# The last pass of the attention scores over 128 rows instead of 64

## The chip, the cores and the metric

The kernel runs on one core of one Trainium2 chip. The metric is the device time of one execution in microseconds; the number of record is the median of the runs, and beside it stands a profiled execution, whose span runs from the program's first instruction to its last.

The engines are named as in the profile: PE is TensorE's matmuls (transposes are matmuls with an identity), PEld its weight loads, DVE is VectorE, ACT is ScalarE, POOL is GpSimd, SP is the engine that issues most DMAs.

## What is computed

The reference is an encoder of two layers over 1024 tokens of 1024 channels in float32. Each layer has a token mixer (attention with four heads beside a depthwise convolution of width 31), an output projection, and a feed-forward part with 16 experts, each of which takes its 128 best tokens. The change lies in the attention. Per head a query and a key have 192 channels: 128 plain ones, and 64 that are rotated by the token's position. In the reference, in short:

```
q = concatenate([q[..., :QK_NOPE_DIM], apply_rope(q[..., QK_NOPE_DIM:], cos, sin)], axis=-1)
k = concatenate([k[..., :QK_NOPE_DIM], apply_rope(k[..., QK_NOPE_DIM:], cos, sin)], axis=-1)
...
s = einsum('bhqd,bhkd->bhqk', q_blk, kt) * scale
p = softmax(s, axis=-1)
return einsum('bhqk,bhkd->bhqd', p, vt)
```

with `QK_NOPE_DIM = 128`, 64 rotated channels, and the same rotated key channels for all heads but for their scale.

## The kernel before

**High and low parts.** Most products take their operands as float32r, which holds fewer bits than float32. So an operand x is kept as a high part, `hi` (x rounded by ScalarE's copy), and a low part, `lo` = x - `hi` (made by VectorE); `split` (L118, L119) does this. A product is three passes of TensorE into the same accumulator, hi hi, lo hi and hi lo (`mm3`, L113 to L115).

**The rotated channels** have only 64 rows, so two of their passes are packed into one of 128 rows. `q_t` (L525) writes `qs`: its rows 0 to 63 are the high part of the rotated query, rows 64 to 127 the low part. `k_t` (L517) writes `kd`, in which the high part of the rotated key stands twice, in rows 0 to 63 and again in 64 to 127, and `kl`, the low part, in rows 0 to 63 alone. Both go through `out_r` (L512): ScalarE copies all 128 rows to `hi` (L514), VectorE subtracts in the rows `r` it is given (L515). For both the source `p2` holds the rotated values twice, in both halves of its rows.

**The scores** of a tile of 128 queries (`scores(u)`, L540) are two halves of 512 keys. For each half there are five passes: three for the plain channels (L113, L114, L115), then `qs` by `kd` over 128 rows (L548: high query by high key, and low query by high key), then rows 0 to 63 of `qs` by rows 0 to 63 of `kl` (L549: high query by low key). A call thus has ten passes, of which two have 64 rows.

**The order of the attention.** Each engine issues in the order in which the program is written; nothing is reordered by a planner. The loop over u (L862) goes over 32 tiles, four heads of eight. In the step of tile u VectorE takes the reciprocal of tile u's sum (L866), and the maximum of tile u + 1's scores (L554, L555); TensorE transposes the probabilities of tile u (`probs_t`, L571, eight transposes in two buffers that ScalarE copies out, L572), and multiplies those of tile u - 1 by the values (`values`, L578); ScalarE takes the exponential of tile u + 1 (L564) behind the copy of the output of tile u - 1 (L579). At the end of the step TensorE does `scores(u + 2)`. So scores, maximum, exponential and transposes of a tile are spread over three steps. Into the steps of the first three heads the next head's queries and keys are woven (`k_mm`, `k_out`, `k_scale`, `k_t`, `q_mm`, `q_out`, `q_rot`, `q_t`; transposes L504, outputs L509, L510, L514, L515), and products of the convolution by VectorE (`give`, L304). Twice a head `values_t` transposes four output tiles and splits them (L118, L119). In the last head there is none of that; in its place come the convolution's layer norm (`ln_in`, transposes L595, statistics by VectorE and three operations of GpSimd; `ln_out` by ScalarE, L606) and the splitting of the output projection's weights (`split_wo`).

Score accumulators (`ps_s`) have two buffers, and so have the two other kinds of accumulators (`ps_t`, `ps_m`).

Of the kernel before, what the change touches and what calls it, by code (L numbers as in the profile page):

```python
# [10 lines left out]
F32 = mybir.dt.float32  # L11
# [9 lines left out]
T, D, KT, TT = 1024, 1024, 8, 8  # L21
# [16 lines left out]
# words per partition of the two arenas  # L38
# [4 lines left out]
def trunk(ctx: ExitStack, tc: tile.TileContext, x, c, positions, norm1_g, w_ada, b_ada, w_in, q_latent_g, w_uq,  # L43
# [10 lines left out]
    ctx.enter_context(tc.manual_schedule())      # each engine issues in the order of this program  # L54
# [5 lines left out]
    # R without the places of two kinds of data, float32 and float32r by turns  # L60
# [15 lines left out]
    class Cut:  # L76
        """[128, 8, n] in two places"""
# [43 lines left out]
    # ---------------------------------------------------------------- constants  # L121
# [17 lines left out]
    # vectors that are needed with their index on the partitions  # L139
# [27 lines left out]
    # columns of b_ada: shift 1, scale 1, shift 2, scale 2  # L167
# [21 lines left out]
    # rotary tables: cos [p, t, 32] and sin with its sign [p, t, (-, +) 32]  # L189
# [31 lines left out]
    # ---------------------------------------------------------------- DRAM scratch  # L221
# [6 lines left out]
    # constants of the router  # L228
# [12 lines left out]
    # ---------------------------------------------------------------- modulation  # L241
    AB = [consts.tile([128, 4, KT], F32, name=f"ab{l}") for l in range(L)]   # scale, shift of the first norm, the second

    def mod_load(l, n, h, raw):
        """rows 512 h .. 512 h + 511 of the columns 512 n .. 512 n + 511 of the modulation of layer l"""
        sp.dma_start(raw, w_ada[l].rearrange("(k p) f -> p k f", p=128)[:, 4 * h:4 * h + 4, 512 * n:512 * n + 512])
# [24 lines left out]
    # ---------------------------------------------------------------- one layer  # L271
    SCR, CB, VB, WRAW, FX = 6144, 8960, 14240, 16288, 28672

    # taps of the depthwise convolution that the parts of the program take
    TAPS = [[1, 0, 2, 0, 2, 2, 2, 1], [1, 1, 2, 1, 1, 1, 0, 1], [3, 6, 5], [4, 4], [0, 0, 7, 9, 7, 5, 5, 8], [5, 6], [5, 6], [0, 0, 8, 8, 6, 4, 6, 5], [[], 0, 1], [0], 1, 1, 0]

    def layer(l):
# [13 lines left out]
        # per token: eps * mean square of the q latent + eps^2, 1 / rms of the kv latent, its square, sum of k rope^2  # L291
        tok = consts.tile([128, 4, TT], F32, name=f"tok{l}", tag="tok")
        RQ = {}
        taps = []                  # depthwise convolution, one product per entry, given out between other work
# [12 lines left out]
        # ---- h = rms_norm(x) * A + B, transposed, in two parts of 512 tokens  # L307
# [23 lines left out]
        # ---- convolution input, gated: y[channel, 15 + token]  # L331
# [27 lines left out]
        # ---- latents: [token, q 256 | kv 128 | k rope 64]  # L359
# [41 lines left out]
        def rotate(dst, src, gr, t0):  # L401
            """dst [128, 4, n, 64] (n copies) = rotated src [128, 4, 64] * gr, for the tokens of tiles t0 .. t0 + 3"""
            xg, xc, xs_ = (fw(o, 4, 64) for o in (SCR + 2304, SCR + 2560, 17280))
            v.tensor_tensor(xg, src, gr[:, None, :].to_broadcast([128, 4, 64]), op=MUL)
            half = lambda ap: ap.rearrange("p t (a b) -> p t a b", a=2)
            v.tensor_tensor(half(xc), half(xg), rc[:, t0:t0 + 4, None, :].to_broadcast([128, 4, 2, 32]), op=MUL)
            v.tensor_tensor(half(xs_), half(xg)[:, :, ::-1], rs[:, t0:t0 + 4], op=MUL)
            if dst.shape[2] == 1:
                v.tensor_tensor(dst[:, :, 0], xc, xs_, op=ADD)
            else:  # L410
                v.tensor_tensor(dst, xc[:, :, None, :].to_broadcast(list(dst.shape)),
                                xs_[:, :, None, :].to_broadcast(list(dst.shape)), op=ADD)
# [5 lines left out]
        # ---- heads  # L418
# [31 lines left out]
        def q_out(hd, grp):  # L450
            st = small.tile([128, 4], F32, name="qst")
            for i in (0, 2):
                a.activation(qr[:, i:i + 2], QS[hd, grp][i // 2][:, :2 * DH].rearrange("p (a b) -> p a b", a=2), AF.Copy)
            for i in range(4):
                jk = small.tile([128, 256], BF16, name="jk", bufs=1)
                a.activation(jk[:, :DH], qr[:, i], AF.Square, accum_out=st[:, i:i + 1])
            tg = slice(4 * grp, 4 * grp + 4)
            # the scale of the exponential carries 1 / sqrt(DH) and 1 / rms(q)
            g.tensor_scalar(st, st, 1.0 / DH, None, op0=MUL)
            g.tensor_tensor(st, st, tok[:, 0, tg], op=ADD)  # L460
            g.tensor_tensor(st, st, neghalf.to_broadcast([128, 4]), op=ALU.pow)
            g.tensor_scalar(RQ[hd][:, tg], st, 1.0 / math.sqrt(DH), None, op0=MUL)
# [54 lines left out]
        def k_t(hd, grp, pool=ps_t):  # L517
            kn, kd, kl, _ = kv_tiles(hd)
            kr, kr2 = kbuf(hd, grp)
            p = to_heads(lambda i: kr[:, i], pool)  # L520
            p2 = to_heads(lambda i: flat(kr2[:, i]), pool)
            out_n(p, kn, grp, c_gk(l))
            out_r(p2, kd, kl, slice(0, 64), grp)
# [10 lines left out]
        # ---- scores, softmax, values  # L534
# [5 lines left out]
        def scores(u):  # L540
            hd, qt = divmod(u, TT)
            kn, kd, kl, _ = kv_tiles(hd)
            qsl = slice(128 * qt, 128 * qt + 128)
            ps = SC[u] = ps_s()
            for n in range(2):
                s = slice(512 * n, 512 * n + 512)
                mm3(ps[:, s], qn[0][:, qsl], qn[1][:, qsl], kn[0][:, s], kn[1][:, s], True, False)
                pe.matmul(ps[:, s], qs[:, qsl], kd[:, s], start=False, stop=False)  # L548
                pe.matmul(ps[:, s], qs[:64, qsl], kl[:64, s], start=False, stop=True)  # L549
# [7 lines left out]
        def exp_table():  # L557
            """an exponential ahead of those that count: the engine loads its table for it"""
            a.activation(small.tile([128, 1], F32, name="ss")[:1], ident[:1, :1], AF.Exp)
# [21 lines left out]
        def values_t(u):  # L581
            """the outputs of the four tiles that end with u, transposed"""
            hd, grp = divmod(u // 4, 2)
            p = to_heads(lambda i: att(u - 3 + i))
            s = slice(512 * grp, 512 * grp + 512)
            split(catA[0][:, hd, s], catA[1][:, hd, s], p)

        # ---- layer norm of the convolution over the channels, swish
# [33 lines left out]
        # ---- output projection  # L622
# [12 lines left out]
        # ================ order: first norm, convolution input  # L635
# [3 lines left out]
        S = [_view(XC["C"], 2048 * i, (4, 512)) for i in range(4)]       # of the first layer  # L639
# [45 lines left out]
        def mod_now():  # L685
            """the next 512 columns; what mod_then() does needs their sums"""
# [108 lines left out]
        # ================ latents  # L795
# [14 lines left out]
        # ================ the rest of the convolution input, first head  # L810
# [50 lines left out]
        # ================ attention  # L861
# [67 lines left out]
        # ================ output projection, residual, second norm, router logits  # L929
# [45 lines left out]
        # weights of the experts, in parts of 2 x 128 rows, of which each is two blocks of 512 columns  # L975
# [8 lines left out]
        # the part that takes the place of another once that is split  # L984
# [9 lines left out]
        # the last ones in halves  # L994
# [26 lines left out]
        def split_lo(c, q):  # L1021
            """the low part of a quarter of the weights, by the tensor engine"""
# [11 lines left out]
        # ---- router: the CAP first tokens of each expert.  The CAP-th largest affinity of an expert is found from  # L1034
        # its eight sorted lists of 128 tokens, merged to the CAP largest.  Lists are sorted in quarters.  Of the
        # lists of two tiles the first lies in the partitions 0 .. 15, the second in 16 .. 31.
# [7 lines left out]
        def bitonic(n, src, nxt, d):  # L1044
            """sorts each bitonic run of 2 d in the first n partitions, downwards"""
# [10 lines left out]
        def sort_tiles(t0, nt, dst=None, dst2=None):  # L1056
            """sorted lists of the tiles t0 .. t0 + nt - 1, 16 partitions each"""
# [30 lines left out]
        def merge(a_, b_, dst, dst2):  # L1088
            """the largest of two lists, 32 partitions"""
            steps.append(lambda: v.tensor_tensor(dst[:32], a_, b_[:, ::-1], op=ALU.max))  # L1090
            return bitonic(32, dst, dst2, 64)
# [19 lines left out]
        def affine(t):  # L1111
            """softmax of the router's logits, rstd * (x A2 Wr) + B2 Wr"""
# [103 lines left out]
        # what a slot takes from its token: index within the tile, tile, affinity in three exact parts  # L1216
# [26 lines left out]
        # slot of a chosen token: the chosen ones before it; of the tokens at the threshold the first ones are chosen.  # L1243
        # before: those at least at the threshold before the token; after: those above it, from the token on
# [52 lines left out]
        # ================ experts  # L1297
# [101 lines left out]
    # ---------------------------------------------------------------- program  # L1399
# [27 lines left out]
```

## Time and profile before

| what | value |
|---|---|
| runs, us | 2357.45, 2357.79, 2359.66 |
| median, us | 2357.79 |
| profiled execution, span, us | 2356.6 |
| what lies around that span, from the median, us | 1.2 |
| TensorE busy, share of the span | 96% |
| VectorE busy, share of the span | 81% |
| ScalarE busy, share of the span | 58% |
| attention of the first layer, us from the span's start | 238 to 456 |
| attention of the second layer, us | 1396 to 1614 |
| mean granted TensorE clock | 0.988 |

The profile gives no device time of its own for the profiled execution; its span is what is compared with the runs. A busy engine is not an engine at its peak: TensorE's matmuls overlap each other, so their durations add up to more than the time that passes. How fast a row of matmuls goes is read from the distance between their starts.

### The profile page before, as it was taken

The numbers are of one execution on the slowest core, as the hardware profiler recorded it, in microseconds if no ns is written. First come the engines' busy times: TensorE is split into PE (matmuls) and PEld (weight loads), VectorE is DVE, ScalarE is ACT, GpSimd is POOL, SyncE is SP. The second block draws the span as 40 slices with busy tenths as digits, with TensorE's granted clock in tenths as the row PEclk, the third lists the DMA queues.
The fourth block names the chain that finished last, engine by engine and source line by source line (L and its number), as shares of the span: only waits on it lengthen the run. The fifth ranks groups of instructions, "written<-read, shape, count | busy, mean of one in ns | idle before, by whom it ended". The sixth has DMA issues, their size and how long they took to land. (4 is left out here: it accounts for less than half of the span.)

```text
span 2356.6 us, 31226 instructions
## 1 busy us (share of the span) xinstructions
PE 2259.5 (96%) x11845; PEld 1789.3 (76%) x11845; DVE 1907.4 (81%) x2648; ACT 1356.9 (58%) x1770; POOL 416.8 (18%) x405
## 2 busy tenths in 40 slices
PE   6999999999999999999969999999989999999997
PEld 3678788787688787878847778877867887787786
DVE  3886888567888999999959868875688889999997
ACT  4324666623667677776741356666246667677675
POOL 1001211201021222313010021121010121331320
PEclk9999999999999999999979999999999999999999
DMA  8472000344899999999946300004358999999996
GB/s 271 157 258 77 13 9 1 109 146 153 302 338 352 371 382 380 373 387 377 354 137 211 131 12 15 1 28 155 116 208 314 344 349 387 379 379 382 373 386 236
DMA packets 179355, 550.97 MB, mean 234 GB/s; under 512 B 12821, under 2 KB 34471, under 8 KB 179205
## 3 DMA queue, kind: packets, MB, share of 16 engines
q1 hardware_dynamic: 169712, 515.35, 59.0%
q0 software_dynamic: 9216, 33.56, 5.6%
q8 instruction: 93, 1.52, 0.3%
q14 instruction: 58, 0.47, 0.1%
q10 hardware_dynamic: 276, 0.07, 0.0%
HBM read 515.35 MB, written 33.59 MB: 233 GB/s over the span
## 5 line engine op out<-in xcount | busy, mean ns | idle before, releaser
L119 DVE TENSOR_TENSOR R<-F,R 128x2048 fp32r<-128x2048 f32 (+1 forms) x294 | 635.9, 2182 | 74.7 <-ACT R L118 74.3
L118 ACT ACTIVATE R<-F 128x2048 fp32r<-128x2048 f32 (+1 forms) x294 | 532.9, 1832 | 71.2 <-DMA F<-in_w_up_dram 26.9
L115 PE MATMUL S<-R,flexX 128*128 128x512 f32 x1096 | 431.9, 394 | 9.8 <-DVE R L119 9.8
L113 PE MATMUL S<-R,flexX 128*128 128x512 f32 x1096 | 439.0, 401 | 0.0
L114 PE MATMUL S<-R,flexX 128*128 128x512 f32 x1096 | 427.3, 390 | 0.0
L304 DVE SCALAR_TENSOR_TENSOR F<-F,cw 128x1024 f32<-128x1024 f32 x240 | 307.4, 1281 | 5.3
L119 DVE TENSOR_TENSOR flexC<-F,flexC 128x2048 fp32r<-128x2048 f32 (+3 forms) x126 | 257.9, 2052 | 16.9 <-ACT flexC L118 16.9
L115 PEld LDWEIGHTS S<-R,flexX 128*128 128x128 f32 x1096 | 205.6, 188 | 64.0 <-DVE R L119 16.8
L118 ACT ACTIVATE flexC<-F 128x2048 fp32r<-128x2048 f32 (+3 forms) x126 | 216.8, 1728 | 47.1 <-DMA F<-in_w_in_dram 14.0
L114 PEld LDWEIGHTS S<-R,flexX 128*128 128x128 f32 x1096 | 206.1, 188 | 42.7
L113 PEld LDWEIGHTS S<-R,flexX 128*128 128x128 f32 x1096 | 206.1, 188 | 39.6 <-ACT flexX L118 0.5
L118 ACT ACTIVATE flexX<-T 128x512 fp32r<-128x512 f32 x128 | 73.1, 597 | 237.3 <-PE T L1314 133.6
L115 PE MATMUL S<-R 128*128 128x512 f32 x480 | 189.9, 396 | 0.0
L113 PE MATMUL S<-flexC,flexX 128*128 128x512 f32 x440 | 176.5, 401 | 0.0
L115 PE MATMUL S<-flexC,flexX 128*128 128x512 f32 x440 | 173.3, 394 | 2.5 <-DVE flexC L119 2.5
L114 PE MATMUL S<-flexC,flexX 128*128 128x512 f32 x440 | 171.8, 390 | 2.4 <-DVE flexX L119 2.4
L1359 POOL DMA_INDIRECT x<-F,idx x16 | 97.7, 6108 | 390.1 <-DVE F L1358 364.8
L1359 POOL DMA_INDIRECT out_dram<-F,idx x16 | 94.7, 5919 | 390.2 <-DVE F L1358 364.8
L578 PE MATMUL m<-F 128*128 128x128 f32 x1024 | 124.8, 275 | 0.0
L113 PE MATMUL S<-R 128*128 128x512 f32 x288 | 123.3, 428 | 0.0
L578 PEld LDWEIGHTS m<-F 128*128 128x128 f32 x1024 | 119.4, 192 | 0.0
L572 ACT ACTIVATE F<-T 128x512 f32<-128x512 f32 x128 | 70.0, 594 | 83.7 <-PE T L571 82.9
(294 smaller groups left out, 4063.4 us busy)
## 6 DMA issues: line engine op xcount, KB each, us to landing
F<-in_w_gate_dram SPq DMA_DIRECT2D x128, 1024.0 KB
F<-in_w_up_dram SPq DMA_DIRECT2D x128, 1024.0 KB
F<-in_w_down_dram SPq DMA_DIRECT2D x126, 1024.0 KB
F<-in_w_ada_dram SPq DMA_DIRECT2D x42, 1024.0 KB
F<-in_x_dram SPq DMA_DIRECT2D x16, 512.0 KB
F<-in_w_in_dram SPq DMA_DIRECT2D x16, 512.0 KB
F<-in_w_out_dram SPq DMA_DIRECT2D x16, 512.0 KB
h<-F SPq DMA_DIRECT2D x16, 512.0 KB
```

Source lines behind the costliest of these rows:

```text
L113: pe.matmul(ps, lh, rh, start=first, stop=False)
L114: pe.matmul(ps, ll, rh, start=False, stop=False)
L115: pe.matmul(ps, lh, rl, start=False, stop=last)
L118: a.activation(hi, src, AF.Copy)
L119: (sub or v.tensor_sub)(lo, src, f32(hi))
L304: taps.append(lambda i=i: v.scalar_tensor_tensor(ACC[j], Y[j][:, i:i + T], w[:, i:i + 1], ACC[j], op0=MUL, op1=ADD))
L572: a.activation(PTS[u % 2][:, 4 * b:4 * b + 4], p.rearrange("p (k q) -> p k q", k=4), AF.Copy)
L578: pe.matmul(po[:, :DV], PTS[u % 2][:, k], V[:, k], start=(k == 0), stop=(k == KT - 1))
L1359: g.indirect_dma_start(out=xm_d, out_offset=bass.IndirectOffsetOnAxis(ap=idx[:, e:e + 1], axis=0), in_=y, in_offset=None, compute_op=ADD)
```

## The change

`k_t` hands `out_r` the rows 0 to 127 in place of 0 to 63, so that VectorE's subtraction writes all 128 rows of `kl`; rows 64 to 127 hold the low part of the rotated key a second time. The last pass of each half in `scores` then takes all 128 rows of `qs` and of `kl`: high query by low key as before, and low query by low key besides. The number of instructions is the same.

```diff
@@ k_t
-            out_r(p2, kd, kl, slice(0, 64), grp)
+            out_r(p2, kd, kl, slice(0, 128), grp)
...
@@ scores
                 mm3(ps[:, s], qn[0][:, qsl], qn[1][:, qsl], kn[0][:, s], kn[1][:, s], True, False)
                 pe.matmul(ps[:, s], qs[:, qsl], kd[:, s], start=False, stop=False)
-                pe.matmul(ps[:, s], qs[:64, qsl], kl[:64, s], start=False, stop=True)
+                pe.matmul(ps[:, s], qs[:, qsl], kl[:, s], start=False, stop=True)
```

Everything else in the diff takes out comments; the line numbers stay.

## Rows read from the trace of the kernel before

**Rows 1.** The page's busy times: busy us, share of the span, instructions.

```profile
PE 2259.5 (96%) x11845; PEld 1789.3 (76%) x11845; DVE 1907.4 (81%) x2648; ACT 1356.9 (58%) x1770; POOL 416.8 (18%) x405
```

**Rows 2.** Stretch, us; busy us (count) of PE, PEld, DVE, ACT, POOL; clock; DMA.

```profile
296.61:355.17 58.56, 58.54 (x385) 47.19 (x384) 48.09 (x73) 36.68 (x92) 9.49 (x18) 1.00 0.00 1
...
1454.98:1513.54 58.56, 58.54 (x385) 47.19 (x384) 48.10 (x73) 36.68 (x92) 9.50 (x18) 1.00 0.00 1
```

**Rows 3.** Timeline of PE: start, us taken, line, out<-in, count.

```profile
345.58 0.39 PE L114 MATMUL S<-flexX,R 128*128 128x512 f32 x1
345.82 0.39 PE L115 MATMUL S<-flexX,R 128*128 128x512 f32 x1
346.05 0.40 PE L548 MATMUL S<-flexX,R 128*128 128x512 f32 x1
346.38 0.49 PE L549 MATMUL S<-flexX,R 64*128 64x512 f32 x1
346.80 0.50 PE L113 MATMUL S<-flexX,R 128*128 128x512 f32 x1
347.14 0.39 PE L114 MATMUL S<-flexX,R 128*128 128x512 f32 x1
...
348.35 1.09 PE L571 MATMUL T<-ident,F 128*128 128x128 f32 x8
349.28 1.95 PE L578 MATMUL m<-F 128*128 128x128 f32 x16
...
355.17 1.09 PE L571 MATMUL T<-ident,F 128*128 128x128 f32 x8
```

**Rows 4.** Timeline of the weight loads; in brackets idle time before, releaser.

```profile
345.59 0.19 PEld L115 LDWEIGHTS S<-flexX,R 128*128 128x128 f32 x1
...
346.38 0.18 PEld L549 LDWEIGHTS S<-flexX,R 64*128 64x128 f32 x1 [0.37 <-issue]
```

**Rows 5.** Weight loads by line and shape: busy us, mean ns | idle before.

```profile
L549 PEld LDWEIGHTS S<-R 64*128 64x128 f32 x96 | 17.5, 183 | 35.0 <-issue 35.0
```

**Rows 6.** Timeline of PE just ahead of the attention.

```profile
224.25 0.40 PE L115 MATMUL S<-R 128*128 128x512 f32 x1
224.48 1.04 PE L504 MATMUL T<-ident,F 128*128 128x128 f32 x8
225.35 1.07 PE L504 MATMUL m<-ident,F 128*128 128x128 f32 x8
```

**Rows 7.** VectorE by line and shape, 232 to 515 us.

```profile
L119 DVE TENSOR_TENSOR R<-T,R 128x512 fp32r<-128x512 f32 x8 | 5.5, 691 | 16.1 <-ACT R L118 16.1
L515 DVE TENSOR_TENSOR R<-T,R 64x512 fp32r<-64x512 f32 x8 | 5.5, 684 | 0.1
```

**Rows 8.** Timeline of VectorE, stretches of heads 1 and 3.

```profile
308.76 0.69 DVE L119 TENSOR_TENSOR R<-T,R 128x512 fp32r<-128x512 f32 x1 [3.46 <-ACT R L118]
...
326.45 1.23 DVE L554 TENSOR_REDUCE st<-S 128x1 f32<-128x1024 f32 x1 [2.30 <-PE S L549]
...
347.19 0.69 DVE L119 TENSOR_TENSOR R<-T,R 128x512 fp32r<-128x512 f32 x1 [0.72 <-ACT R L118]
...
424.91 0.69 DVE L119 TENSOR_TENSOR R<-T,R 128x512 fp32r<-128x512 f32 x1 [3.47 <-ACT R L118]
```

**Rows 9.** Timeline of ScalarE, same stretches.

```profile
353.13 0.19 ACT L564 ACTIVATION_READ_ACCUMULATOR F<-S,st,rq 128x1 f32 x1
...
428.65 0.78 ACT L606 ACTIVATE F<-m,mv 128x512 f32<-128x512 f32 x1 [0.30 <-POOL mv L601]
```

**Rows 10.** Waits of VectorE in head 1: total us, times, longest.

```profile
DVE st L554 <- PE S L549: 2.8, 2, 2.3
```

**Rows 11.** Busy time by stretch, elsewhere; granted clock behind POOL's.

```profile
455.00:470.00 15.00, 11.89 (x83) 9.83 (x82) 6.78 (x13) 11.82 (x19) 3.71 (x6) 1.00 0.63 209
...
602.43:609.26 6.83, 6.77 (x40) 3.74 (x39) 3.65 (x21) 1.64 (x2) 1.23 (x1) 0.50 0.43 145
```

**Rows 12.** Waits of PE in the first layer's attention.

```profile
PE m L595 <- ACT F L606: 1.5, 1, 1.5
```

## The prediction

> **What bounds the kernel now.** The page's busy line comes first: TensorE is busy for 96% of the span [rows 1]. That share mixes stages, and the change touches one of them, the attention, so the next view is the table of busy time by stage, cut at the heads (a head's eight query tiles, from the first transposes of its probabilities on). A head takes 58.56 us, TensorE is busy in 58.54 of them and VectorE in 48.09; the second layer's row is the same to 0.02 us [rows 2]. TensorE is never without work there, so time taken out of its stream is time gained, as long as VectorE (82% busy) and ScalarE keep up.
>
> A busy share does not say how fast TensorE goes, because pipelined matmuls overlap. For that one reads the starts in the order of time. In the ten passes of one call of `scores`, three passes of 128 rows follow each other at 0.24, 0.23 us [rows 3]. The last pass of each half has 64 rows (64x512), and around it the rhythm breaks: it starts 0.33 us after the pass before it (346.05 to 346.38), the pass behind it starts 0.42 us later (346.80), and the one after that 0.34 us later (347.14). The weight loads say why: a 128-row load begins while an earlier matmul runs (345.59, one step ahead of its own pass at 345.82), but the load of the 64-row pass begins together with its matmul, 346.38, after 0.37 us with no load at all, charged to "issue", which is no other engine [rows 4]. All 128 such passes do it; of 96 of them the loads' idle time is 35.0 us, 0.365 us each, and the other 32 have the same rate [rows 5].
>
> **The change, part by part.** (1) The pass gets 128 rows of weights and of keys, like its neighbours. Its cost in the new form is not in the trace of before under its own line, but 128x512 passes that end a product and are followed by transposes are: in the work just before the attention one starts at 224.25, the transposes behind it at 224.48, 0.23 us later, and those eight take 0.87 us up to the next group's start [rows 6]. So I price the new pass at 0.23 us ahead of it and 0.23 us behind it. The gain at each pass is 0.33 - 0.23 = 0.10 us ahead and 0.42 - 0.23 = 0.19 us behind. After the first half the next pass's 0.34 becomes 0.23: 0.11. After the second half the eight transposes, 0.93 us from 348.35 to 349.28 [rows 3], become 0.87: 0.06. Sum for a call: 2 x 0.29 + 0.11 + 0.06 = 0.75 us. There are 128 passes, so 64 calls: **48.0 us** if nothing else holds TensorE back. The other end of this price is that the new pass keeps the old gaps and nothing is gained; I take the first, because rows of the same shape and type are the nearest there are.
>
> That 128-row loads hide behind 128-row matmuls is what the sum stands on, and the rows show it: the load of 345.59 runs under the matmul that began at 345.58 and took 0.39 us [rows 3, 4]. The Trainium skill says the opposite (TensorE: Matmul & The Clock Gate, The mechanism): a weight load overlaps running matmuls only where the row groups differ. By that rule the 128-row load would stay in the open, 0.23 + 0.19 = 0.42 us, as behind the 64-row pass today, and the sum would be zero; this trace disagrees, and I go by the trace.
>
> (2) `k_t` makes the low part for 128 rows instead of 64: a VectorE subtraction of 128x512 instead of 64x512, 16 times (four heads, two halves, two layers). The 64-row one takes 684 ns, a 128-row subtraction from the same kind of buffer 691 ns [rows 7]: 0.1 us in all. It is the same instruction at the same place with the same predecessors, so it adds no wait; the score pass already waits for it. Were it to cost as much again as today, it would be 16 x 0.68 = 11 us of VectorE, which is TensorE's only where VectorE is late. I take 0.1 us.
>
> (3) What is late next. TensorE comes 0.75 us earlier per call; what VectorE and ScalarE do between two of its uses stays. The maximum of the scores (L554), the exponential (L564) and the transposes of the probabilities (L571) are a chain over three engines, one tile ahead. I follow it where VectorE has least room, around the end of a head. VectorE is tied to TensorE at 308.76, where it has waited 3.46 us for a ScalarE copy (L118 in `values_t`) behind transposes that TensorE made ahead of tile 11's scores. From there to the transposes of tile 16's probabilities at 355.17 [rows 3] TensorE does seven calls of `scores` (tiles 11 to 17), so it would come 7 x 0.75 = 5.25 us earlier. VectorE's waits on the way that can shrink are 2.30 (for scores, 326.45) and 0.72 us (347.19), 3.02 in all; the exponential's sum is read at 353.13 + 0.19 = 353.32, 1.85 us ahead of the transposes [rows 8, 9]. So TensorE waits 5.25 - 3.02 - 1.85 = 0.4 us there. One such place for each of three heads and two layers: 2.3 us. In the last head there is a second chain: VectorE's subtraction at 424.91 (tied to TensorE by a wait of 3.47 us), the statistics behind it, GpSimd's three operations, ScalarE's `ln_out` at 428.65, which already waits 0.30 us for them, and TensorE's next transposes L595, which need the buffer that it frees [rows 8, 9]. One call of `scores` lies between, so that wait grows by 0.75 us, which I count in full: 1.5 us in two layers. Everything behind the attention (output projection, router, experts, with their weight loads) starts when places of the attention come free, so it moves along as a whole.
>
> **Sum.** -48.0 + 2.3 + 1.5 + 0.1 = -44.1 us. The profiled execution spans 2356.6 us from first to last instruction; the median of the timed runs is 1.2 us more, and I leave that distance as it is: 2357.8 - 44.1 = **2313.7 us**, a span of 2312.5.
>
> **Rivals.** *VectorE becomes the bound.* After the change a head would need 58.56 - 6.0 = 52.6 us of TensorE, and VectorE is busy for 48.09, 91% of that. Of its waits in that head only 2.8 us are for scores [rows 10]; the others name ScalarE or GpSimd. If those do not shrink, a head takes 58.56 - 2.8 = 55.8 us, six heads give 16.8 us, the last heads 2 x 6.0 - 1.5 = 10.5 us: 2330.5 us. For it: the high share. Against it: its longest wait, 3.46 us, is for a ScalarE copy that follows TensorE. It decides from some 10 us of TensorE waits for L564 in the first three heads on.
>
> *Nothing is gained.* The gaps would belong to the place of the pass (the last of its group, before another bank) and not to its 64 rows; or, by the page's rule above, the load would not be hidden. 2357.8 us. Against it: the 128-row pass at 224.25 is the last of its group too, and has no gap [rows 6].
>
> *Slower: the clock.* TensorE gets waits in its stream where it had almost none. If they let the clock fall to the lower of its levels (1.2 GHz), a stretch as the one at 602 us, 6.83 us at 0.50 with TensorE busy [rows 11], costs half of it, 3.4 us. From 13 such stretches on (44 / 3.4) the gain is gone; one for every second of 64 tiles would be 32 x 3.4 = 109 us, or 2313.7 + 109 = 2423 us. Against it: TensorE already waits 1.5 us once at the end of the attention [rows 12], and the clock of that stretch, 455 to 470 us, stays at 1.00 [rows 11].
>
> **Chances and range.** The forecast has 0.83, VectorE as the bound 0.12, no gain 0.03, the clock 0.02. No stall at all would give 2309.7 us; half-rate stretches behind the attention, whose places can shift, add or take some 2 us: low end 2307. Stalls four times those I found (15 instead of 3.8 us) give 2325, the high end; the range leaves out the rivals' times and holds the forecast's case nearly whole. Some 0.2% (4.7 us) is what a measurement of this kernel can tell from no change. Faster by more than that: 0.95; within: 0.03; slower: 0.02.
>
> **What the profile after would show.** Right: L549 as 128x512, starting 0.23 us after its predecessor and followed after 0.23 us; its weight load with no idle time; a call of `scores` up to the next transposes at about 2.3 us instead of 3.09; heads of about 53 us; VectorE at over 90% in the first three heads, its waits for scores (now at L554 after L549) almost gone; TensorE with short new waits for L564 at the heads' ends. Step 1 is wrong if the gaps around L549 are still there. Step 2 is wrong if L515 over 128 rows takes clearly more than 0.69 us. Step 3 is wrong if TensorE's waits in the attention sum to over 10 us, or if L595 gets no longer wait. The forecast as a whole fails if the stages behind the attention take longer than before although nothing in them is changed.

## The result and the profile after

The changed kernel takes 2317.2 us (median of 4 runs, 2317.1 to 2317.7) beside 2358.1 us for the kernel before in the same session: a ratio of 0.983, 95% interval 0.9816 to 0.9844, or 40.9 us less (36.8 to 43.4 by the interval). The forecast was 2313.7 us, 44.1 less, in a range of 2307 to 2325. The profiled executions span 2315.3 and 2356.6 us, 41.3 apart.

The page's busy line of the changed kernel, which answers to [rows 1]:

```profile
PE 2216.0 (96%) x11845; PEld 1798.5 (78%) x11845; DVE 1906.7 (82%) x2648; ACT 1357.0 (59%) x1770; POOL 430.0 (19%) x405
```

The shares hardly move, though 41 us are gone: TensorE has 43.5 us less of recorded busy time, and the other engines' busy times change little. What changed is seen in the starts. The timeline of PE over one call of `scores` in the changed kernel, to be held against [rows 3]:

```profile
286.61 0.48 PE L113 MATMUL S<-R 128*128 128x512 f32 x1
286.93 0.39 PE L114 MATMUL S<-R 128*128 128x512 f32 x1
287.16 0.39 PE L115 MATMUL S<-R 128*128 128x512 f32 x1
287.39 0.40 PE L548 MATMUL S<-R 128*128 128x512 f32 x1
287.62 0.39 PE L549 MATMUL S<-R 128*128 128x512 f32 x1
287.85 0.40 PE L113 MATMUL S<-R 128*128 128x512 f32 x1
288.09 0.39 PE L114 MATMUL S<-R 128*128 128x512 f32 x1
...
288.77 0.39 PE L549 MATMUL S<-R 128*128 128x512 f32 x1
289.00 1.03 PE L571 MATMUL T<-ident,F 128*128 128x128 f32 x8
290.12 0.38 PE L578 MATMUL m<-F 128*128 128x128 f32 x1
```

L549 now has the shape of its neighbours and keeps their rhythm: 0.23 us behind L548 (it was 0.33), the next pass 0.23 us behind it (0.42), the one after that 0.24 (0.34). The weight loads, by line and as a timeline, against [rows 4, 5]:

```profile
L549 PEld LDWEIGHTS S<-R 128*128 128x128 f32 x96 | 18.0, 188 | 4.1
```

```profile
287.16 0.19 PEld L548 LDWEIGHTS S<-R 128*128 128x128 f32 x1
287.39 0.19 PEld L549 LDWEIGHTS S<-R 128*128 128x128 f32 x1
```

The load of L549 starts at 287.39, one pass ahead of its matmul at 287.62, and the idle time before these 96 loads falls from 35.0 to 4.1 us. VectorE's wider subtraction costs nothing that can be seen; the instructions of L515, in ns (least, median, most), the 12 of 128x512 and the 8 of 64x512 from one kind of buffer together:

```profile
L515 DVE TENSOR_TENSOR R<-T,R x20: 678/682/694, 220.6 to 1523.5; 128x512 fp32r<-128x512 f32 x12, 64x512 fp32r<-64x512 f32 x8
```

Busy time by stretch in the changed kernel: heads 0 to 2 of the first layer, and head 3 up to its last tile (columns as in [rows 2]). In the second layer heads 0 to 2 agree with this to 0.03 us, and head 3 is 0.16 us shorter.

```profile
234.92:289.00 54.08, 52.07 (x373) 46.94 (x372) 48.45 (x73) 38.36 (x101) 14.34 (x22) 1.00 0.06 17
289.00:342.83 53.83, 53.62 (x386) 48.35 (x384) 47.95 (x72) 36.44 (x93) 9.63 (x18) 1.00 0.02 7
342.83:396.61 53.78, 53.59 (x386) 48.34 (x384) 48.13 (x71) 36.42 (x92) 11.02 (x18) 1.00 0.00 1
396.61:435.16 38.55, 36.93 (x265) 33.53 (x263) 22.82 (x41) 27.04 (x47) 9.83 (x18) 1.00 0.24 83
```

Head 1 went from 58.56 to 53.83 us. VectorE's busy time in it is the same (47.95 against 48.09), so its share is now 89%. Where VectorE and TensorE wait in the changed kernel, VectorE in head 1 and TensorE over the first layer's attention and shortly behind it, against [rows 10, 12]:

```profile
DVE R L119 <- ACT R L118: 2.0, 1, 2.0
...
DVE st L554 <- PE S L549: 0.4, 1, 0.4
```

```profile
PE m L595 <- ACT F L606: 2.3, 2, 1.5
PE T L571 <- DVE R L510: 1.8, 1, 1.8
PE T L571 <- ACT F L564: 0.8, 1, 0.8
PE T L571 <- DVE R L119: 0.6, 1, 0.6
```

In the kernel before, L571's wait for L510 was shorter; and the new wait of L595 is at 411.53 in the changed kernel:

```profile
PE T L571 <- DVE R L510: 1.1, 1, 1.1
```

```profile
411.53 0.66 PE L595 MATMUL m<-ident,F 128*128 128x128 f32 x4 [0.85 <-ACT F L606]
```

VectorE's wait for scores fell from 2.8 to 0.4 us a head: it is no longer ahead of TensorE. L595 waits 2.3 us in place of 1.5: the engine is idle for 0.85 us before it at 411.53, and from the start of the matmul ahead of it to its own start 0.75 us more pass than before (1.12 against 0.37), which is the size that was forecast there. L571 waits 1.8 us for VectorE's L510 once, 0.7 us more than before; that was not forecast. Not all that TensorE loses stands in this list. At the end of each head a wait falls inside a group of transposes; the timelines of VectorE and of PE at tile 7:

```profile
280.05 2.60 DVE L304 SCALAR_TENSOR_TENSOR F<-F,cw 128x1024 f32<-128x1024 f32 x2
282.56 0.68 DVE L119 TENSOR_TENSOR R<-T,R 128x512 fp32r<-128x512 f32 x1
```

```profile
282.56 1.40 PE L571 MATMUL T<-ident,F 128*128 128x128 f32 x8
283.79 0.50 PE L578 MATMUL m<-F 128*128 128x128 f32 x3
```

The eight transposes take 1.23 us up to the next line's start instead of 0.93. Their second half needs the accumulator buffer that `values_t` filled, and VectorE's L119 reads it only from 282.56 on, behind two products of the convolution. A shorter wait follows one tile later, for another VectorE operation: the eight transposes of 289.00 are followed by L578 after 1.12 us, because its first product needs a buffer that L510 reads from 289.31 to 290.06.

### The profile page after: what moved, and what is told of

It is laid out like the page before. It is cut to its first block, busy times and chain, and to the rows that moved or that the text cites. A ratio compares the mean times of both kernels' runs of the same rounds, so it can differ in the third digit from the quotient of the medians.

```text
span 2315.3 us, 31226 instructions
## 1 busy us (share of the span) xinstructions
PE 2216.0 (96%) x11845; PEld 1798.5 (78%) x11845; DVE 1906.7 (82%) x2648; ACT 1357.0 (59%) x1770; POOL 430.0 (19%) x405
## 5 line engine op out<-in xcount | busy, mean ns | idle before, releaser
L119 DVE TENSOR_TENSOR R<-F,R 128x2048 fp32r<-128x2048 f32 (+1 forms) x294 | 636.5, 2185 | 74.7 <-ACT R L118 74.3
L119 DVE TENSOR_TENSOR flexC<-F,flexC 128x2048 fp32r<-128x2048 f32 (+3 forms) x126 | 258.3, 2055 | 16.5 <-ACT flexC L118 16.4
L115 PE MATMUL S<-R 128*128 128x512 f32 x480 | 189.5, 395 | 0.0
L578 PE MATMUL m<-F 128*128 128x128 f32 x1024 | 125.2, 275 | 0.3
L578 PEld LDWEIGHTS m<-F 128*128 128x128 f32 x1024 | 119.4, 192 | 1.2 <-DVE R L510 1.2
L113 PE MATMUL S<-R 128*128 128x512 f32 x288 | 118.3, 411 | 0.0
L114 PE MATMUL S<-R 128*128 128x512 f32 x288 | 112.6, 391 | 0.0
```

The lines of the kernel that those rows point to most:

```text
L113: pe.matmul(ps, lh, rh, start=first, stop=False)
L114: pe.matmul(ps, ll, rh, start=False, stop=False)
L115: pe.matmul(ps, lh, rl, start=False, stop=last)
L119: (sub or v.tensor_sub)(lo, src, f32(hi))
L578: pe.matmul(po[:, :DV], PTS[u % 2][:, k], V[:, k], start=(k == 0), stop=(k == KT - 1))
```

## The experiments

All were run beside the kernel before, and the ratio given is to that one.

**1. The low part alone.** The theory is that everything comes from the shape of the last pass. So the first edit was kept and the second taken back:

```diff
-                pe.matmul(ps[:, s], qs[:, qsl], kl[:, s], start=False, stop=True)
+                pe.matmul(ps[:, s], qs[:64, qsl], kl[:64, s], start=False, stop=True)
```

> Only the first half of the change: the key's low part is made for 128 rows, the last pass stays at 64 rows. Theory (the whole gain comes from the pass's shape on TensorE): nothing to be gained or lost, 2358 us as before (within 1 us), VectorE's 16 subtractions at 0.68 to 0.69 us each. Rival (the wider subtraction takes or gives something of its own): over 2 us away from 2358.

Ratio 1.0004, interval 0.9995 to 1.0014; its profiled execution spans 2358.0 us. Heads 0 to 2 of its first layer take 58.84, 58.57 and 58.56 us, before's 58.85, 58.57 and 58.58. So the wider subtraction gives or takes nothing in the attention; of the whole the interval says this to 3 us (the medians are 1.6 us apart, where 1 us was expected).

**2. One half of the call.** 128 rows in the first half, 64 in the second:

```diff
-                pe.matmul(ps[:, s], qs[:, qsl], kl[:, s], start=False, stop=True)
+                r = slice(0, 128) if n == 0 else slice(0, 64)
+                pe.matmul(ps[:, s], qs[r, qsl], kl[r, s], start=False, stop=True)
```

> The last pass has 128 rows in the first half of each scores call and 64 rows in the second. Theory (each 64-row pass pays for entering and leaving its shape, one by one): 0.40 us less for each of 64 calls, 25.6 us, less some 2 us of new waits for late buffers: 2334 us, range 2331 to 2337. Rival (the gap comes once for a call, at its end, where the transposes follow): under 10 us, over 2348.

2335.1 us beside 2360.3, 25.2 less, ratio 0.989 (0.9874 to 0.9907). The timeline of PE in this kernel, where the last pass is L550:

```profile
302.20 0.40 PE L548 MATMUL S<-R 128*128 128x512 f32 x1
302.44 0.39 PE L550 MATMUL S<-R 128*128 128x512 f32 x1
302.67 0.40 PE L113 MATMUL S<-R 128*128 128x512 f32 x1
...
303.36 0.39 PE L548 MATMUL S<-R 128*128 128x512 f32 x1
303.68 0.50 PE L550 MATMUL S<-R 64*128 64x512 f32 x1
304.11 1.10 PE L572 MATMUL T<-ident,F 128*128 128x128 f32 x8
```

The same line of the program keeps the rhythm with 128 rows (0.24, 0.23 us) and breaks it with 64 (0.32, 0.43). Both are the last of their group; so it is the rows and not the place, and each pass pays for itself.

**3. The 64-row passes side by side.** Before's passes in another order, so that the second half begins with its 64-row pass:

```diff
+                if n == 1:
+                    pe.matmul(ps[:, s], qs[:64, qsl], kl[:64, s], start=True, stop=False)
-                mm3(..., True, False)
-                pe.matmul(ps[:, s], qs[:, qsl], kd[:, s], start=False, stop=False)
-                pe.matmul(ps[:, s], qs[:64, qsl], kl[:64, s], start=False, stop=True)
+                mm3(..., n == 0, False)
+                pe.matmul(ps[:, s], qs[:, qsl], kd[:, s], start=False, stop=(n == 1))
+                if n == 0:
+                    pe.matmul(ps[:, s], qs[:64, qsl], kl[:64, s], start=False, stop=True)
```

> Before's ten passes with before's 64 rows, in another order: the second half begins with its 64-row pass, so the two 64-row passes of a call stand side by side. Theory (the price is in the change between 64 and 128 rows, ahead and behind): one entry and one exit for a call in place of two, the pair 0.23 us apart with the second load hidden, 0.35 us less for each call, 22 us less about 1 us of new waits: 2337 us. Rival 1 (a 64-row weight load is never hidden, whatever stands ahead of it): the pair is 0.42 us apart, 0.16 us less for each call: 2348 us. Rival 2 (the last place in the group costs it): the second pass, no longer last, loses its gaps wherever it stands, the first keeps them.

2341.1 us beside 2360.3, 19.1 less, ratio 0.9922 (0.9905 to 0.9938); the profiled execution is 19.5 us shorter than that of before. Timelines of PE and of the weight loads:

```profile
302.74 0.39 PE L550 MATMUL S<-R 128*128 128x512 f32 x1
303.06 0.49 PE L552 MATMUL S<-R 64*128 64x512 f32 x1
303.39 0.39 PE L548 MATMUL S<-R 64*128 64x512 f32 x1
303.72 0.50 PE L113 MATMUL S<-R 128*128 128x512 f32 x1
304.05 0.40 PE L114 MATMUL S<-R 128*128 128x512 f32 x1
```

```profile
303.06 0.18 PEld L552 LDWEIGHTS S<-R 64*128 64x128 f32 x1 [0.36 <-issue]
303.17 0.19 PEld L548 LDWEIGHTS S<-R 64*128 64x128 f32 x1
303.71 0.19 PEld L113 LDWEIGHTS S<-R 128*128 128x128 f32 x1 [0.36 <-issue]
```

The second 64-row load starts at 303.17, ahead of its matmul at 303.39, without idle time; a load of the same shape is hidden. Loads wait only where the shape changes, at 303.06 and 303.71. So one entry and one exit per call are saved, as the theory says, and the time (0.30 us a call over 64 calls) is nearer to its 22 us than to rival 1's 10. Rival 2 is refuted too: the second pass, now first of its group, still has an exit of 0.33 us. The distances were not those expected: the pair is 0.33 us apart, not 0.23, and the exit takes 0.33, not 0.42. The sum is: from 302.74 to 304.05 the pair costs 1.31 us, 0.39 more than four steps of 0.23, and a lone pass in [rows 3] costs 1.09 us, 0.40 more than three such steps. Why it is shared out in this way stays open.

**4. The pass left out.** Who binds the attention now? The pass of query by low key is dropped, and with it the part of the scores that the key's low part adds on the rotated channels:

```diff
-                pe.matmul(ps[:, s], qs[:, qsl], kd[:, s], start=False, stop=False)
-                pe.matmul(ps[:, s], qs[:, qsl], kl[:, s], start=False, stop=True)
+                pe.matmul(ps[:, s], qs[:, qsl], kd[:, s], start=False, stop=True)
```

> The last pass of each half (rotated query by low key) is left out altogether. It asks who binds the attention after the change. If TensorE alone did: 128 passes of 0.23 us less than the changed kernel, 29.6 us, 2317.2 - 29.6 = 2288. Theory (VectorE is next: in a head of the first three it is busy 48 us and has some 3.6 us of waits that don't follow TensorE): those heads go from 53.8 to about 51.7 us, the last ones lose 8 x 0.46 us, together 20 us: 2297 us, with waits of TensorE for VectorE and ScalarE that sum to about 10 us in the attention.

2311.6 us, ratio 0.9797 (0.978 to 0.9813): 48.6 us under before, only some 8 us more than the change itself. My figure of 2297 was far off. Head 1's stretch in this kernel, VectorE's three longest waits in it, and TensorE's longest waits in the first layer's attention (lines are one lower from L549 on):

```profile
288.00:341.13 53.13, 50.87 (x369) 45.17 (x369) 47.92 (x72) 36.53 (x93) 11.62 (x18) 1.00 0.03 10
```

```profile
DVE R L119 <- ACT R L118: 1.9, 1, 1.9
DVE flexX L510 <- ACT flexX L509: 0.9, 1, 0.9
DVE R L510 <- ACT R L509: 0.8, 1, 0.8
```

```profile
PE T L570 <- DVE R L119: 3.7, 6, 0.8
PE T L570 <- DVE R L510: 3.0, 4, 2.0
```

With 16 passes fewer a head still takes 53.13 us, against 53.83. VectorE's 47.92 us and its waits for ScalarE and GpSimd, 4.5 us in the whole list, make that time up nearly in full. The changed kernel stands almost on this floor, which holds for VectorE's work in this order: I had put it at 51.7, because I took VectorE's wait of L119 for one that shrinks.

**5. VectorE's load taken away.** To price VectorE's lateness, the convolution's products are left out of the attention's loop, in the changed kernel and in the kernel before; the changed one ran again beside them.

```diff
-            give(TAPS[0][i])
...
-                give(len(taps) if hd == NH - 2 and i == 7 else TAPS[1][i])
```

> The changed kernel once more, beside the three that follow, so that they are compared on one chip: 2317 us, 41 us under before.

> The changed kernel with the convolution's products (taps) left out of the attention's loop, about 93 VectorE operations of 1.28 us in each layer; so VectorE is never late there. Theory (the 6 us that are missing from the calls' full worth are TensorE's waits for a late VectorE): against the kernel before without taps the change is worth the calls' full 64 x 0.73 = 47 us, less the last head's 0.75 us in each layer: 45.5 us. Rival (the waits come from ScalarE's and GpSimd's chain, or the shorter passes disturb something else): the difference stays at 41 us as with the taps.

> The kernel before with the same taps left out. Theory (TensorE binds the attention before the change, VectorE does not): about 2357 us, at most 2 us under before, from waits of TensorE of 1.1 us in each layer. Rival (VectorE binds before as well): over 10 us less.

The kernel before: 2357.1 us; without the products 2357.5 (ratio 0.9999, 0.999 to 1.0008). Some 136 us of VectorE work (53 operations of 1.28 us in a layer, not the 93 of the expectation) are gone without a change of time, and heads 0 to 2 take 58.84, 58.57 and 58.58 us, as with them: before the change VectorE's load did not set the attention. The changed kernel again: 2318.6 us (0.9831); without the products 2314.9 (0.9814, 0.9799 to 0.9829). So the late VectorE costs the changed kernel 3.7 us by the medians; heads 0 to 2 give 4.9 us for both layers (below). Head 1 without the products, in the changed kernel:

```profile
288.15:341.22 53.07, 53.05 (x386) 48.45 (x384) 27.02 (x54) 36.80 (x93) 7.02 (x18) 1.00 0.02 7
```

53.07 us against 58.56: (58.56 - 53.07) / 8 = 0.69 us a call with VectorE idle half the time. By the medians the change is worth 42.6 us there, between the rival's 41 and the 45.5 expected; heads 0 to 2, 53.06 to 53.10 us without the products and 53.78 to 54.08 with them, speak against the rival. Yet even without a late VectorE a call is not worth the 0.73 us of the expectation. The starts, compared pair by pair over head 1 against before, show what is left: 4.65 us at L549, 0.85 at the pass behind it, 0.25 in the transposes, and 0.23 given back ahead of and in the values' products (L578).

**6. The same work in another order.** If late buffers are the cause, a tap moved to where VectorE idles should give the time back.

```diff
-            give(TAPS[0][i])
+            give(TAPS[0][i] - (i == 6 and not last) + (i == 1 and 0 < hd < NH - 1))
...
+            if last and i == 1:
+                ln_in(1)
             if i == 6 or (i == 1 and hd):
                 values_t(u - 2 - (i == 6))
...
-                give(len(taps) if hd == NH - 2 and i == 7 else TAPS[1][i])
+                give(len(taps) if hd == NH - 2 and i == 7 else 0 if u == 1 else TAPS[1][i] + (u == 4))
...
-                ln_in(i)
+                if i != 1:
+                    ln_in(i)
...
             if u == 1:
                 q_t(0, 1)
+                give(TAPS[1][1])
```

> The changed kernel with all its work, in another order at four places: in heads 0 to 2 one of the two taps of the seventh step goes to where VectorE idles (in head 0 to the fifth step, in the next two to the second step, ahead of a 2.04 us wait); the tap of the second tile goes behind the second query group's transposed output; in the last head the second tile's layer norm statistics go ahead of the outputs' transposes. Theory (the waits are for buffers that a late VectorE frees, and VectorE has idle time nearby): in each layer 0.7 us at tile 2, 0.6 us at each of three head ends, 0.75 us in the last head, 6 us in both layers: 2311 us. Rival (VectorE has no time left, the waits come back at another tile): 2316 to 2317 us.

2316.7 us (0.9816, 0.9802 to 0.9831), not 2311. In the attention the theory holds for the most part: from the first transposes of probabilities to the last, a layer takes 199.7 us where the changed kernel takes 201.8, so 4.1 us in two layers. TensorE's wait for L595 of 0.85 us is gone; a new one of 0.63 us stands in head 0 where its tap went. The stages behind the attention took 1.3 to 2.2 us more in the first layer than in the two profiled executions of the changed kernel, and 1.8 us more in the second. The next kernel moved head 0's tap once more, `TAPS[1][i] + (u == 4)` back to `TAPS[1][i]` and, in the latents' loop:

```diff
-            give(TAPS[3][more])
+            give(TAPS[3][more] + (t == 7))
```

> The kernel with the moved taps, and head 0's tap not into its fifth step (where a new wait of 0.63 us stood) but ahead of the attention, into the last of the eight latent tiles. Theory: the attention of each layer 0.6 us shorter than with the taps moved first, 199.1 us instead of 199.7, from the first to the last transposes of probabilities; the whole, if the stages behind the attention take what they took in the changed kernel (937 to 938 us up to the next layer's first transposes, 739.5 us after the last ones), 2312 us. Rival: the stages behind it take 2 us more again, 2315 to 2316 us.

2314.7 us (2313.0 to 2316.5; ratio 0.9817, 0.9804 to 0.9831). The attention gets shorter again, 198.5 us in a layer, twice the 0.6 us expected and 6.6 in all under the changed kernel, which is the size forecast for these waits. Head 1:

```profile
288.01:341.09 53.08, 53.06 (x385) 48.45 (x384) 47.93 (x72) 36.33 (x94) 11.22 (x18) 1.00 0.02 5
```

With all of VectorE's work (47.93 us) the head takes what it took without the convolution's products, 53.07 us. So the waits came from the order of VectorE's work and not from its amount. The whole does not follow: 2.5 us less than the changed kernel's 2317.2, with intervals that overlap. Is it faster than the changed kernel? Likely, not shown.

**7. The same, a little later.** In the last kernel of experiment 6, eight or sixteen transposes of the identity ahead of the first layer's scores shift all that follows (`range(2 ...)` for sixteen):

```diff
+        for _ in range(1 if l == 0 else 0):
+            pad = ps_t()
+            for i in range(8):
+                pe.transpose(pad[:, 128 * (i % 4):128 * (i % 4) + 128], ident, ident)
         scores(0)
```

> The same with eight transposes of the identity, about 0.9 us of TensorE, ahead of the first layer's scores; they shift all that follows and feed nothing. Theory (the half-rate stretches of the router's stage fall where the arrival time puts them, and cost by it): the attention is the same to 0.2 us, the whole changes by something other than +0.9 us, with a different sum of half-rate time between 555 and 615 us or 1690 and 1730 us. Rival (the stages behind the attention take the same, whenever they begin): +0.9 us, 0.2 either way, and the same half-rate sums.

> The same with sixteen such transposes, about 1.75 us. Theory as for eight: not +1.75 us. Rival: +1.75 us, 0.2 either way.

2316.7 us (2314.8 to 2319.2) and 2313.9 us (2313.4 to 2316.5), beside 2314.7 without: +2.0 and -0.8, neither +0.9 nor +1.75, but the runs overlap, so the medians decide nothing. In the profiled executions the stretch from the first layer's last transposes to the second layer's first, without a pad and with sixteen transposes ahead:

```profile
433.44:1376.09 942.65, 901.39 (x4414) 716.98 (x4413) 783.37 (x1054) 531.63 (x543) 172.59 (x103) 0.98 0.77 278
```

```profile
435.99:1373.81 937.82, 898.02 (x4414) 715.04 (x4413) 782.68 (x1054) 531.40 (x544) 168.40 (x103) 0.98 0.77 280
```

The same stages with the same work take 942.65 us in one and 937.82 in the other. The router's stage, 555 to 615 us, without a pad, with eight and with sixteen transposes:

```profile
555.00:615.00 60.00, 52.91 (x256) 34.87 (x254) 46.52 (x158) 34.16 (x31) 5.75 (x14) 0.89 0.72 256
```

```profile
555.00:615.00 60.00, 55.86 (x266) 36.76 (x264) 47.66 (x168) 36.16 (x32) 5.73 (x13) 0.89 0.73 269
```

```profile
555.00:615.00 60.00, 54.63 (x267) 36.70 (x265) 48.30 (x169) 36.93 (x34) 6.12 (x14) 0.91 0.75 273
```

A granted clock of 0.89 means 2 x (1 - 0.89) x 60 = 13 us at half rate, 0.91 means 11. From 1690 to 1730 us the clock is 0.83 in all three. So with eight transposes the half-rate sums of the two stretches that the expectation names are the same as without, as its rival has it, and with sixteen one of them differs. Another stretch differs that the expectation does not name, 1335 to 1350 us, without a pad and with sixteen:

```profile
1335.00:1350.00 15.00, 12.80 (x62) 10.65 (x61) 10.36 (x17) 5.98 (x17) 4.14 (x8) 0.89 0.08 23
```

```profile
1335.00:1350.00 15.00, 12.80 (x74) 10.77 (x73) 10.98 (x20) 5.67 (x18) 3.46 (x7) 1.00 0.09 23
```

That the arrival time decides this is not shown. Each of these kernels was profiled once, and the five runs without a pad, which nothing shifts against each other, have mean granted clocks of 0.984 to 0.988; the profiled one is the 0.984. Low-clock time thus differs between executions of one kernel, and that rival is left standing.

## Why the prediction was right, and where it was off

**The pass (step 1).** Right in mechanism: distances and hidden load came as priced, and experiments 1 to 3 leave the shape of the pass as the cause. Mis-sized: 0.75 us a call. With VectorE out of the way a layer's heads 0, 1 and 2 are 5.8, 5.5 and 5.5 us shorter (58.85, 58.57 and 58.58 before), the last 3.75 us with 0.75 us of new wait in it, and the two calls ahead of them bring 1.49 (0.74 each, as their starts show): 22.0 + 0.75 = 22.8 us for 32 calls, **0.71 us**. Over 64 calls 45.6 us in place of 48.0. The term that was mis-sized is the transposes behind the second half: in head 1 the distances at L549 give 4.65 / 8 = 0.58 us a call and the pass behind it 0.85 / 8 = 0.11, as priced, but the 0.06 us of the transposes came to nothing (0.25 us gained in them and 0.23 lost at L578, in eight calls). The rule of the Trainium skill that stood beside this step (TensorE: Matmul & The Clock Gate, The mechanism) is not borne out as it was quoted: the load of 287.39 runs under the 128-row matmul that began at 287.39. The same section also has loads into a background weight buffer pulled ahead of running matmuls, which would agree; no run here shows into which buffer a load goes.

**The subtraction (step 2).** Right: 0.68 us an instruction, no effect that can be seen on the time (experiment 1).

**What is late next (step 3).** The last head's wait came as forecast, 0.75 us a layer. The late VectorE was mis-sized: 2.3 us forecast; heads 0 to 2 take 54.08, 53.83 and 53.78 us with the convolution's products and 53.06, 53.07 and 53.10 without, 2.45 us a layer, **4.9 us**. It was also misplaced. I followed the exponential, and in these heads no wait of TensorE for it is listed; TensorE waits for accumulator buffers that VectorE frees late, in L119 of `values_t` at the head's end and in L510 at tile 2, which the prediction put at nothing. Start by start against the kernel without the products, 0.65 of the 2.45 us lie at tile 2 and 0.87 inside the transposes of the three heads' last tiles; the rest is in smaller waits.

**The sum.** -45.6 + 1.5 + 4.9 = -39.2 us in the attention. Outside it the profiled execution is 2.1 us shorter, 1.3 of them ahead of the first scores, where nothing was changed. The errors of 2.4 and 2.6 us, both to the slow side, were partly made up by this, and that is luck: the first scores start at 229.0 us in the profiled execution of the kernel before, at 228.2 with experiment 1's edit and at 227.7 in the changed kernel. That the stages behind the attention move along as a whole held to some 1 us here; in the kernels with moved taps they took up to 5 us more (942.65 us against the changed kernel's 937.45). In the prediction's range, the time without stalls is 2313.7 - 3.8 = 2309.9 us and not 2309.7; nothing hangs on it.

**The rivals.** No gain: refuted by the result, and its reason, the place of the pass, by experiment 2. The clock in the attention: 1.00 in all stretches. VectorE as the bound: not yet, but by little. In this order of the work its floor is 53.1 us a head (experiment 4), the changed kernel's heads take 53.8, and TensorE alone would need 53.07. The two are about level now: in experiment 4 sixteen passes fewer took 0.7 us off a head. Whether the order of experiment 6 would lower that floor was not tried.

## What to carry to other kernels

A pass with fewer rows need not be cheaper: here one of 64 rows among neighbours of 128 cost more than a full one. Look at the distances between starts around it and at where its weight load begins, and fill the rows if the operand is there anyway, even with work that nobody asked for. When a saving repeats inside a loop in which another engine is over 80% busy, follow that engine's waits to see which are really tied to the engine that gets faster, and follow the buffers it frees, not only the data it makes. A few microseconds gained in one stage can be lost behind it, so a small change is judged by its own stage's stretch and by more than one execution.

## What was not expected of the hardware

The price of a lone 64-row pass, 0.10 us ahead, 0.19 behind and 0.11 at the pass after that, is more than the 0.23 us for which a full pass runs; two of them side by side together pay about as much as one (0.39 us against 0.40, experiment 3), and there the exit is 0.33 us where a lone pass has 0.42.

Stretches at TensorE's lower clock in the router's stage, where TensorE waits 1 to 2 us at several places, come at other places and in other numbers from one profiled execution to the next. In those with moved taps the stretch between the layers' attentions took 937.8 to 942.7 us, with the same instructions. Neither the arrival time as the cause nor the clock as the whole of that difference is shown: most of the time at half rate in that stretch, 20 to 24 us, lies around 1167 to 1192 us, where TensorE stands idle for up to 16 us at a time.
